# Moving modulation columns, key copies, spilled tiles and gate transposes in a two-block transformer kernel

## The chip, the cores and the metric

One core of a Trainium2 chip runs the whole kernel. The metric is the device time of one execution in microseconds, as a median over timed runs.

## The reference

Two transformer blocks are computed on a sequence of 512 rows of width 1024, in float32.

```python
c_act = silu(c)
for layer in range(2):
    mod = c_act @ ada_w[layer] + ada_b[layer]
    sh_m, sc_m, g_m, sh_f, sc_f, g_f = split(mod, 6)
    h = modulate(rms_norm(x, pre_mix_g), sh_m, sc_m)
    y = gmlp_mixer(h) if layer == 0 else fox_mixer(h, k, v, dcum)
    x = x + g_m * rms_norm(y, post_mix_g)
    h = modulate(rms_norm(x, pre_ffn_g), sh_f, sc_f)
    y = (silu(h @ w_gate) * (h @ w_up)) @ w_down
    x = x + g_f * rms_norm(y, post_ffn_g)
    if layer == 0:
        k, v, dcum = shared_kv(x, c_act @ kv_ada_w + kv_ada_b)
```

The hidden width of the FFN is 2816. `shared_kv` normalises and modulates x, multiplies it with the key, value and forget weights and normalises the keys per head. The second block follows: products for an mLSTM with four heads and for a sparse attention with eight heads whose keys an indexer picks, an output product, a gate, and a last norm.

## The kernel before

**Products.** Each float32 matrix is held as a high part (float32r, made by ScalarE) and a low part (the rest, made by VectorE's or GpSimd's subtraction). A product of two such matrices takes three matmuls (`mm3`, L414 to L416). `wsplit` (L277, L280) loads a weight chunk of 128x1024 from DRAM into one of four `raw` buffers and splits it into `whi` and `wlo`, each with four buffers; with `share=n`, GpSimd makes the low half of every n-th chunk. `gemm_a` keeps weights stationary and works output block by output block; one chunk is 24 matmuls of 128x512. `gemm_b` keeps the activations stationary: per group of 512 output columns it holds four accumulators, one for each 128 rows, and goes through chunks of 256 rows of the weight, 24 matmuls each. Its argument `then` runs a function after the first chunk of a group; `tail` chunks at the end are worked off row block by row block.

**Modulation columns.** `mod` is made column by column on VectorE: each of 112 columns is a load of 128x1024 (`ada_load`, L296, on SyncE's queue) and one multiply with sum over the free axis (`ada`, L300) into `modc`. Sixteen are made at the start. The other 96 go in the order of the list `ADA` and are spread over the products by `fill(n)`, which loads n columns into `raw` buffers per call and works off the columns loaded one earlier. In the first FFN's `gemm_a` each chunk from the eleventh on calls `fill(2)`; what is left is drained in a loop before the down product. The output product of the mixer, a `gemm_b`, calls `fill(1.5)`. `need` drains until eight named columns are there.

**FFN.** `ffn` multiplies with gate and up blocks in turn (`gemm_a`, 44 chunks). `evac` applies silu, multiplies (L603) and splits the result (L546, L548). Then `gemm_b` with the down weights follows, two groups of eleven chunks, with `post` as evacuation: norm, residual, norm of the next stage, and from every second row block transposes into `hk` (`to_T`). For the first FFN `to_T` also writes the normalised rows, transposed, to DRAM (`xT`, the spill).

**Shared keys and values.** `gemm_b` with the key weights (`headnorm` evacuates: L886 square, L888 sum, L889 copy, then a scaling of four tiles), then `forget` (L1111), then the eight spilled tiles: each is loaded from `xT` into a T tile (L1126), modulated on ScalarE (L1127), copied and subtracted on VectorE (L1128, L1129). Then `gemm_b` with the value weights. `kdone` transposes four pairs of heads, splits them into T tiles (L1082, L1083) and writes them with `spread` from GpSimd's queue (L941): each half (64 partitions) of the high and low tile is written twice, so that DRAM holds four ready tiles of 128x512 for each pair of heads. There are nine T tiles. `loader` (L953) fetches these tiles on SyncE for this pair and the next. The second block's attention does the same with six tiles per pair (`ev_a`, L1292, L1293, L941).

**Attention.** For each head: scores (L990, L991), softmax, transposes (L1017), values (L1032), with chunks of other products between them.

**Gates.** After the index product, a chain of small operations with two scans (L1264 to L1273) makes the gates `la` and `lt` in T tiles. `columns()` transposes the index weights (L1253) and then the gates (L1259), and is called after the first of the `w_aqk` chunks; the index scores (L1309 to L1317) follow the second.

**Order.** Each engine takes its instructions in a fixed order, settled when the program is built; a scheduler settles it from the program's order and its own costs, except in the parts that are written under a manual schedule. SyncE and GpSimd take their DMA issues in order too.

Of the kernel before, what the change touches and what calls it, by code (L numbers as in the profile page):

```python
# [40 lines left out]
GU = (2, 3)  # L41
GG = (1, 1)
DT = (4, 4)
DS = (0, 0)
# [3 lines left out]
IG = 1  # L48
# [141 lines left out]
def body(tc, nc, a):  # L190
    V, S_, G, PE = nc.vector, nc.scalar, nc.gpsimd, nc.tensor

    with ExitStack() as es:
# [99 lines left out]
        def ada_load(col, raw=None):  # L293
# [124 lines left out]
        def gemm_a(h, w, n, evac, m=P, group=0, nfill=0, share=0, gshare=1):  # L418
# [38 lines left out]
        def gemm_b(h, w, groups, kt, evac, head=False, tail=0, nfill=0, share=0, raws=(), hshare=1, then={}):  # L457
# [6 lines left out]
            for gi in groups:  # L464
# [125 lines left out]
        def ffn(l, h, xsrc, xdst, gb, nxt):  # L590
            with tc.tile_pool(name=f"f{l}", bufs=44) as pf:
# [346 lines left out]
        def spread(d, at, hi, lo):  # L938

            for q, (src, half) in zip(at, ((hi, TOP), (lo, TOP), (hi, BOT), (lo, BOT))):  # L940
                nc.gpsimd.dma_start(d[q].rearrange("(a p) n -> p a n", a=2),  # L941
                                    src[half].unsqueeze(1).broadcast_to((64, 2, 512)))

        def loader(alloc, src, n, last):
# [697 lines left out]
```

## Time and profile before

| | |
|---|---|
| Median of three timed runs | 1885.8 us |
| Lowest and highest | 1879.63 and 1886.22 us |
| Profiled execution | 1873.39 us, span 1871.5 us |
| Mean granted TensorE clock | 0.994 |
| TensorE busy | 1822.3 us (97%) |
| VectorE, ScalarE, GpSimd busy | 1126.0, 789.9, 357.9 us |
| DMA | 305.76 MB, 163 GB/s |

In the rows further down PE is TensorE's matmul, PEld its weight load, DVE is VectorE, ACT ScalarE, POOL GpSimd and SP SyncE; a small q behind the name is the engine's own queue of instructions. "out<-in" names the tiles that an instruction writes and reads, `<-` behind a wait names what ended it, and x counts instructions. Times are microseconds unless a row says ns.

### The profile page before, as it was taken

What the parts mean: (1) busy time and instruction counts of PE and PEld (TensorE: products, weight loads), DVE (VectorE), ACT (ScalarE), POOL (GpSimd) and SP (SyncE); (2) the same over time, 40 slices, a digit from 0 to 9 for tenths busy, and PEclk for the clock granted to TensorE, in tenths of its full rate; (3) what the DMA queues carried; (4) which work ended last, traced back from release to release, by engine and by line L of the source; (5) the groups of instructions that cost most, each with busy time, mean ns of one, the idle gap of its engine ahead of it and who ended that gap; (6) DMA issues with size and microseconds to landing.
All of it is one profiled execution on the core that took longest, in us unless ns stands there. A gap on an engine that the chain in (4) does not pass through costs nothing. (4 is left out here: it accounts for less than half of the span.)

```text
span 1871.5 us, 23902 instructions
## 1 busy us (share of the span) xinstructions
PE 1822.3 (97%) x8688; PEld 1504.1 (80%) x8688; DVE 1126.0 (60%) x2166; ACT 789.9 (42%) x1395; POOL 357.9 (19%) x294
## 2 busy tenths in 40 slices
PE   8999999999999999999999999999999999999997
PEld 5788888888777877787778888888887878888886
DVE  7869745577774256549876423332278978746534
ACT  5333324422222244558765322322256256455334
POOL 2000000222220023343331211100012562031022
PEclk9999999999999999999999999999999999999999
DMA  9674563587775437745533332332436553333532
GB/s 341 234 251 144 159 230 113 171 268 242 253 260 189 147 120 232 259 168 163 165 102 113 112 102 90 101 112 91 147 130 193 176 164 123 106 96 107 173 110 78
DMA packets 101969, 305.76 MB, mean 163 GB/s; under 512 B 12278, under 2 KB 13086, under 8 KB 101851
## 3 DMA queue, kind: packets, MB, share of 16 engines
q1 hardware_dynamic: 93402, 276.96, 44.7%
q0 software_dynamic: 8448, 27.27, 4.1%
q8 instruction: 69, 1.13, 0.2%
q14 instruction: 50, 0.40, 0.1%
HBM read 269.50 MB, written 37.30 MB: 164 GB/s over the span
## 5 line engine op out<-in xcount | busy, mean ns | idle before, releaser
L277 ACT ACTIVATE whi<-raw 128x1024 fp32r<-128x1024 f32 x281 | 296.7, 1058 | 644.2 <-PE acc L416 303.4
L280 DVE TENSOR_TENSOR wlo<-raw,whi 128x1024 fp32r<-128x1024 f32 x191 | 238.3, 1251 | 303.8 <-ACT whi L277 285.0
L414 PE MATMUL acc<-h,whi 128*128 128x512 f32 x896 | 350.5, 391 | 3.2 <-DVE t L603 2.6
L416 PE MATMUL acc<-h,wlo 128*128 128x512 f32 x896 | 349.5, 390 | 4.1 <-DVE wlo L280 4.0
L280 POOL TENSOR_TENSOR wlo<-raw,whi 128x1024 fp32r<-128x1024 f32 x90 | 221.7, 2465 | 673.0 <-ACT whi L277 593.7
L415 PE MATMUL acc<-h,whi 128*128 128x512 f32 x896 | 348.9, 389 | 0.0
L414 PE MATMUL acc<-whi,h 128*128 128x512 f32 x608 | 242.2, 399 | 8.8 <-DVE h L406 5.2
L415 PE MATMUL acc<-wlo,h 128*128 128x512 f32 x608 | 240.3, 396 | 1.4 <-POOL wlo L280 1.1
L416 PE MATMUL acc<-whi,h 128*128 128x512 f32 x608 | 240.1, 396 | 0.0
L416 PEld LDWEIGHTS acc<-h,wlo 128*128 128x128 f32 x896 | 168.2, 188 | 41.7 <-DVE wlo L280 6.6
L414 PEld LDWEIGHTS acc<-h,whi 128*128 128x128 f32 x896 | 168.3, 188 | 40.0 <-issue 5.3
L415 PEld LDWEIGHTS acc<-h,whi 128*128 128x128 f32 x896 | 168.3, 188 | 34.5
L300 DVE SCALAR_TENSOR_TENSOR raw<-raw,cact 128x1024 f32<-128x1024 f32 x96 | 146.4, 1536 | 76.7 <-DMA raw<-in_ada 73.9
L414 PE MATMUL acc<-whi,s 128*128 128x512 f32 (+1 forms) x488 | 190.6, 391 | 0.6 <-DVE t L1328 0.6
L415 PE MATMUL acc<-wlo,s 128*128 128x512 f32 (+1 forms) x488 | 190.9, 391 | 0.3 <-DVE wlo L280 0.3
L416 PE MATMUL acc<-whi,s 128*128 128x512 f32 (+1 forms) x488 | 190.2, 390 | 0.0
L414 PEld LDWEIGHTS acc<-whi,h 128*128 128x128 f32 x608 | 115.5, 190 | 33.6 <-DVE h L406 6.4
L416 PEld LDWEIGHTS acc<-whi,h 128*128 128x128 f32 x608 | 115.6, 190 | 26.0 <-DVE h L407 2.0
L415 PEld LDWEIGHTS acc<-wlo,h 128*128 128x128 f32 x608 | 115.7, 190 | 25.5 <-POOL wlo L280 1.9
L572 POOL DMA_DIRECT2D scr<-s x24 | 13.3, 556 | 541.5 <-DVE s L571 540.4
L414 PEld LDWEIGHTS acc<-whi,s 128*128 128x128 f32 x488 | 91.7, 188 | 20.4 <-DVE t L1328 1.0
L415 PEld LDWEIGHTS acc<-wlo,s 128*128 128x128 f32 x488 | 91.7, 188 | 19.3 <-DVE wlo L280 0.6
(371 smaller groups left out, 2779.4 us busy)
## 6 DMA issues: line engine op xcount, KB each, us to landing
raw<-in_ada SPq DMA_DIRECT2D x96, 512.0 KB, 4.1
raw<-in_w_gu SPq DMA_DIRECT2D x88, 512.0 KB, 4.0
raw<-in_w_dn SPq DMA_DIRECT2D x44, 512.0 KB, 3.4
scr<-t POOLq DMA_DIRECT2D x56, 256.0 KB, 5.6
raw<-in_w_o SPq DMA_DIRECT2D x20, 512.0 KB, 3.3
row<-scr SPq DMA_DIRECT2D x36, 256.0 KB, 2.7
d<-in_ada SPq DMA_DIRECT2D x16, 512.0 KB, 6.9
raw<-in_w_v SPq DMA_DIRECT2D x16, 512.0 KB, 4.7
```

The lines of the kernel that those rows point to most:

```text
L277: S_.activation(hi[:, 0:n], raw[:, 0:n], AF.Copy)
L280: e.tensor_sub(lo[:, 0:n], raw[:, 0:n], hi[:, 0:n].bitcast(F32))
L300: V.scalar_tensor_tensor(raw, raw, 1.0, cact[0], ALU.mult, ALU.mult, accum_out=modc[:, col:col + 1])
L414: PE.matmul(out, lh, rh, start=start, stop=False)
L415: PE.matmul(out, lh, rl, start=False, stop=False)
L416: PE.matmul(out, ll, rh, start=False, stop=stop)
L572: nc.gpsimd.dma_start(xdst[rows, h * 512:(h + 1) * 512], xr[h])
```

## The change

- **First FFN, gate and up.** VectorE makes all low halves (`GU[0]` from 2 to 0), and `fill` gets 1.625 columns per chunk instead of 2.
- **First FFN, down.** The loop that drained the rest of the columns moves from before the product into the evacuation's first call of `mod` (second group, first row block). The product calls `fill(1.5)`; its columns are loaded as two half tiles of 128x512 out of the H tiles, three columns ahead, and take two instructions and a sum.
- **Keys.** The high and low tile of a pair are written to DRAM whole, once (two writes instead of four). The loader puts the four (or six) tiles together out of half-tile loads.
- **Spilled tiles.** Three loads are issued before the value product; the modulation of two tiles goes behind the second and the third chunk of each of its two groups, and loads the next ones.
- **Gates.** The gates' transposes leave `columns()` and are called after the fourth `w_aqk` chunk instead of the first.
- Unused arguments (`gshare`, `DS`) go.

```diff
-GU = (2, 3)
+GU = (0, 3)
@@ ada_load, ada, fill
+        def ada_load(col, raw=None, half=None):
+            if half:
+                raw = [half(), half()]
+                for q in range(2):
+                    nc.sync.dma_start(raw[q], a["ada"][col][:, q * 512:(q + 1) * 512])
+                return col, raw
...
         def ada(col, raw):
+            if isinstance(raw, list):
+                s = small()
+                for q in range(2):
+                    V.scalar_tensor_tensor(raw[q], raw[q], 1.0, cact[0][:, q * 512:(q + 1) * 512], ALU.mult, ALU.mult,
+                                           accum_out=s[:, q:q + 1])
+                V.tensor_add(modc[:, col:col + 1], s[:, 0:1], s[:, 1:2])
+                return
...
-        def fill(n=1):
+        def fill(n=1, half=None, depth=1):
...
-                    held.append(ada_load(ADA[ada_next[0]]))
-                if len(held) > 1 or ada_next[0] >= len(ADA) and held:
+                    held.append(ada_load(ADA[ada_next[0]], half=half))
+                if len(held) > depth or ada_next[0] >= len(ADA) and held:
@@ gemm_b
-                    if 0 < c < nch - 1:
-                        fill(nfill)
+                    if 0 < c < nch - (2 if half else 1):
+                        fill(nfill, half, 3 if half else 1)
                     for t in range(NT):
                         part(t, c, wh, wl)
                     if c == 0 and gi in then:
                         then[gi]()
+                    if each:
+                        each(c)
@@ ffn
-                gemm_a(h, a[f"w_gu{l}"], 2 * KF, evac, group=4, nfill=2, share=GU[l], gshare=GG[l])
-                while len(done) < len(ADA):
-                    fill()
+                gemm_a(h, a[f"w_gu{l}"], 2 * KF, evac, group=4, nfill=1.625, share=GU[l])
                 gb = gb()
-                gemm_b((hh, hl), a[f"w_dn{l}"], range(2), KF, post(gb, xsrc, xdst, F, nxt()), tail=DT[l], share=DS[l])
+                gemm_b((hh, hl), a[f"w_dn{l}"], range(2), KF, post(gb, xsrc, xdst, F, nxt()), tail=DT[l], nfill=1.5, half=None if l else lambda: H(F32))
@@ nxt0
-            hk.extend(hpair())
-            return halves(hk, lambda: (gain(104, "kvg"), need(96)), xT)
+            def mod():
+                while len(done) < len(ADA):
+                    fill()
+                hk.extend(hpair())
+                return gain(104, "kvg"), need(96)
+            return halves(hk, mod, xT)
@@ loader, kdone
-                        for q in range(n):
-                            nc.sync.dma_start(got[p_][q].bitcast(F32), src[p_, q])
+                        for q, half, s in src(p_):
+                            nc.sync.dma_start(got[p_][q][half].bitcast(F32), s)
...
+        def keys(d, at):
+            return [(at[2 * hv + q], ot, d[q, me]) for hv, me in enumerate((TOP, BOT)) for q in range(2) for ot in (TOP, BOT)]
...
-                    spread(kscr[pr], range(4), hi.bitcast(F32), lo.bitcast(F32))
+                    for q, part in enumerate((hi, lo)):
+                        nc.gpsimd.dma_start(kscr[pr, q], part.bitcast(F32))
@@ spilled tiles
-            for j in range(KD):
-                f = T()
-                nc.sync.dma_start(f, xT[j])
-                S_.activation(f, f, AF.Identity, scale=gm[:, j:j + 1], bias=sm[:, j:j + 1])
-                V.tensor_copy(hx[0][j], f)
-                V.tensor_sub(hx[1][j], f, hx[0][j].bitcast(F32))
+            def unspill(c):
+                if c in (0, 3):
+                    return
+                for _ in range(2):
+                    j = len(hdone)
+                    hdone.append(j)
+                    f = spilled[j]
+                    S_.activation(f, f, AF.Identity, scale=gm[:, j:j + 1], bias=sm[:, j:j + 1])
+                    V.tensor_copy(hx[0][j], f)
+                    V.tensor_sub(hx[1][j], f, hx[0][j].bitcast(F32))
+                    if len(spilled) < KD:
+                        spill_load()
+            hdone = []
+            for _ in range(3):
+                spill_load()
             gemm_b(hk, a["w_vv"], range(2), KD, lambda g, t, pt: vsplit(g, t, pt, va, vdone),
-                   then={0: lambda: kdone(1)})
+                   then={0: lambda: kdone(1)}, each=unspill)
@@ ev_a
+                for q, part in enumerate((hi, lo)):
+                    nc.gpsimd.dma_start(d[2 * (i % 2) + q], part)
                 if i == 0:
                     columns()
+                if i == 3:
+                    gates_T()
```

## Rows read from the trace of the kernel before

**Rows 1.** Page, part 1: each engine's busy time, share of the span, instructions.

```profile
PE 1822.3 (97%) x8688; PEld 1504.1 (80%) x8688; DVE 1126.0 (60%) x2166; ACT 789.9 (42%) x1395; POOL 357.9 (19%) x294
```

**Rows 2.** Windows: stretch, its length, busy time (instructions), granted clock, DMA share, GB/s.

```profile
core 0: us, PE busy (x) PEld busy (x) DVE busy (x) ACT busy (x) POOL busy (x), PEclk, DMA share, GB/s
233.00:266.00 33.00, 33.00 (x148) 27.31 (x147) 15.08 (x20) 6.37 (x6) 0.00 (x0) 1.00 0.75 256
374.00:467.60 93.60, 93.60 (x414) 77.54 (x413) 71.30 (x92) 24.91 (x32) 21.25 (x8) 1.00 0.80 255
490.00:570.00 80.00, 73.15 (x308) 56.69 (x308) 60.76 (x80) 19.55 (x26) 14.41 (x6) 1.00 0.79 259
571.00:680.00 109.00, 108.73 (x479) 89.27 (x479) 33.94 (x35) 29.63 (x40) 0.34 (x1) 1.00 0.41 137
```

**Rows 3.** Waits of TensorE, 470 to 570 us: total, times, longest.

```profile
PE acc L416 <- DVE wlo L280: 4.0, 5, 1.0
PE acc L414 <- DVE t L603: 2.6, 5, 1.3
```

**Rows 4.** Timeline of GpSimd and VectorE, 484 to 512 us: start, duration, instruction.

```profile
484.67 2.40 POOL L280 TENSOR_TENSOR wlo<-raw,whi 128x1024 fp32r<-128x1024 f32 x1 [10.18 <-ACT whi L277]
497.25 2.41 POOL L280 TENSOR_TENSOR wlo<-raw,whi 128x1024 fp32r<-128x1024 f32 x1 [10.18 <-ACT whi L277]
510.04 2.41 POOL L280 TENSOR_TENSOR wlo<-raw,whi 128x1024 fp32r<-128x1024 f32 x1 [10.38 <-ACT whi L277]
...
484.75 3.40 DVE L300 SCALAR_TENSOR_TENSOR raw<-raw,cact 128x1024 f32<-128x1024 f32 x1 [0.20 <-DMA raw<-in_ada]
491.50 1.22 DVE L300 SCALAR_TENSOR_TENSOR raw<-raw,cact 128x1024 f32<-128x1024 f32 x1 [0.20 <-DMA raw<-in_ada]
495.77 1.22 DVE L280 TENSOR_TENSOR wlo<-raw,whi 128x1024 fp32r<-128x1024 f32 x1
```

**Rows 5.** Waits of SyncE's queue, 330 to 580 us.

```profile
SPq L296 <- DVE raw L300: 134.6, 57, 3.3
```

**Rows 6.** Timelines of SyncE, ScalarE and TensorE, 728 to 753 us.

```profile
739.60 9.90 SPq L1126 DMA_DIRECT2D t<-scr  x4
...
744.01 0.82 ACT L1127 ACTIVATE t<-t,modc,gcol 128x512 f32<-128x512 f32 x1 [8.61 <-DMA t<-scr]
751.73 0.58 ACT L889 ACTIVATE k<-acc 128x512 f32<-128x512 f32 x1
...
752.36 0.80 PE L414 MATMUL acc<-whi,h 128*128 128x512 f32 x1 [3.54 <-ACT k L889]
```

**Rows 7.** Windows around the lower clock, columns as in rows 2.

```profile
752.00:753.50 1.50, 1.14 (x3) 0.95 (x4) 1.50 (x3) 1.50 (x4) 0.00 (x0) 0.50 1.01 350
753.50:758.00 4.50, 4.50 (x12) 3.53 (x11) 4.12 (x9) 4.50 (x9) 0.00 (x0) 0.50 0.73 255
```

**Rows 8.** Waits of TensorE, 1410 to 1428 us.

```profile
PE tp L1259 <- DVE t L1269: 2.2, 1, 2.2
```

**Rows 9.** Groups of instructions by line: busy us, mean ns, idle before.

```profile
L571 DVE SCALAR_TENSOR_TENSOR s<-t,sm,s 128x512 f32<-128x512 f32 x24 | 17.2, 748 | 0.5 <-DVE sm L358 0.3
```

**Rows 10.** DMA issues: count, KB each, median us to landing.

```profile
scr<-t POOLq DMA_DIRECT2D x56, 256.0 KB, 5.6
scr<-s POOLq DMA_DIRECT2D x24, 256.0 KB, 2.5
k<-scr SPq DMA_DIRECT2D x32, 256.0 KB, 4.5
scr<-t POOLq DMA_DIRECT2D x16, 128.0 KB, 3.5
```

**Rows 11.** SyncE, 820 to 985 us: its waits, and the last key loads.

```profile
SPq L953 <- PE tp L991: 20.8, 7, 6.9
...
909.00 3.68 SPq L953 DMA_DIRECT2D k<-scr  x4
920.86 0.32 SPq L953 DMA_DIRECT2D k<-scr  x1
```

More of the change, by code (lines that the diff above doesn't have):

```diff
@@ L47 @@
 OS = 3
-IG = 1
 MQ = 0
@@ L416, in mm3, with gemm_a @@
             PE.matmul(out, ll, rh, start=False, stop=stop)
-        def gemm_a(h, w, n, evac, m=P, group=0, nfill=0, share=0, gshare=1):
+        def gemm_a(h, w, n, evac, m=P, group=0, nfill=0, share=0):
             hi, lo = h
@@ L455, in gemm_a, with gemm_b @@
                 i += len(run)
-        def gemm_b(h, w, groups, kt, evac, head=False, tail=0, nfill=0, share=0, raws=(), hshare=1, then={}):
+        def gemm_b(h, w, groups, kt, evac, head=False, tail=0, nfill=0, share=0, raws=(), hshare=1, then={}, each=None, half=None):
             hi, lo = h
@@ L936, in stack @@
             return s0, s1
[L938 to L942, printed above, removed]
         def loader(alloc, src, n, last):
@@ L1083, in kdone @@
                     V.scalar_tensor_tensor(lo, pt, kgain[:], hi.bitcast(F32), ALU.mult, ALU.subtract)
-                    spread(kscr[pr], range(4), hi.bitcast(F32), lo.bitcast(F32))
-            kload = loader(lambda dt: tile_of(px, "k", dt, bufs=NKB), kscr, 4, 8)
+                    for q, part in enumerate((hi, lo)):
+                        nc.gpsimd.dma_start(kscr[pr, q], part.bitcast(F32))
+            kload = loader(lambda dt: tile_of(px, "k", dt, bufs=NKB), lambda pr: keys(kscr[pr], range(4)), 4, 8)
             def va(q, t):
@@ L1123, in body, with spill_load @@
             gm, sm = gain(56, "pmg1"), need(48)
[L1124 to L1129 removed]
+            spilled = []
+            def spill_load():
+                spilled.append(T())
+                nc.sync.dma_start(spilled[-1], xT[len(spilled) - 1])
+            def unspill(c):
[13 more added lines that the diff above has]
+                spill_load()
             gemm_b(hk, a["w_vv"], range(2), KD, lambda g, t, pt: vsplit(g, t, pt, va, vdone),
[L1131 removed]
+                   then={0: lambda: kdone(1)}, each=unspill)
             def qa(g, t):
@@ L1241, in ev_ix @@
                     V.tensor_scalar_add(gt[0][64:128], pt[64:128], vc("bgate", 0)[64:128, :])
-            gemm_a(h, a["w_ix"], 5, ev_ix, group=4, gshare=IG)
+            gemm_a(h, a["w_ix"], 5, ev_ix, group=4)
             g = gt[0]
@@ L1254, in columns @@
                 V.tensor_copy(iw[:], pt[:, 0:48].rearrange("p (t h) -> p t h", t=NT)[:, :, 4:12])
-                pt = tp()
-                for q, src in enumerate((la, lt)):
-                    for t in range(NT):
-                        o_ = (q * NT + t) * 4
-                        PE.transpose(pt[:, o_:o_ + 4], src[0:4, t * P:(t + 1) * P], ident[0:4, 0:4])
-                V.tensor_copy(am[:], pt[:, 0:32].rearrange("p (q t h) -> p q t h", q=2, t=NT))
-                S_.activation(am[:, 1, :, :], am[:, 1, :, :], AF.Exp, scale=-1.0)
             lf, lt, la, lm, on = T(), T(), T(), T(), T()
@@ L1275, in body, with gates_T @@
             am = pc.tile([P, 2, NT, 4], F32, name="am")
+            def gates_T():
+                pt = tp()
+                for q, src in enumerate((la, lt)):
+                    for t in range(NT):
+                        o_ = (q * NT + t) * 4
+                        PE.transpose(pt[:, o_:o_ + 4], src[0:4, t * P:(t + 1) * P], ident[0:4, 0:4])
+                V.tensor_copy(am[:], pt[:, 0:32].rearrange("p (q t h) -> p q t h", q=2, t=NT))
+                S_.activation(am[:, 1, :, :], am[:, 1, :, :], AF.Exp, scale=-1.0)
             av = {}
@@ L1288, in ev_a @@
                 d = ascr[i // 2]
-                if i % 2 == 0:
-                    for q, half in enumerate((TOP, BOT)):
-                        ot = (BOT, TOP)[q]
-                        nc.gpsimd.dma_start(d[3 * q, half], hi[half])
-                        nc.gpsimd.dma_start(d[3 * q, ot], lo[half])
-                else:
-                    spread(d, (1, 2, 4, 5), hi, lo)
+                for q, part in enumerate((hi, lo)):
+                    nc.gpsimd.dma_start(d[2 * (i % 2) + q], part)
                 if i == 0:
                     columns()
+                if i == 3:
+                    gates_T()
             gemm_a(h, a["w_aqk"], 2, ev_a, share=2)
@@ L1378, in ev_z, with qsrc @@
                 nc.sync.dma_start(gscr[t, g], s)
-            qkload = loader(qk2, ascr, 6, 4)
+            def qsrc(pr):
+                d = ascr[pr]
+                return ([(0, TOP, d[0, TOP]), (0, BOT, d[1, TOP]), (3, BOT, d[0, BOT]), (3, TOP, d[1, BOT])]
+                        + keys(d[2:4], (1, 2, 4, 5)))
+            qkload = loader(qk2, qsrc, 6, 4)
             def aprep(pr):
```

7 lines of the change are left out of this document (2 added, 5 removed).

## The prediction

> **What bounds the kernel now.** I read the page's first part first: TensorE is busy 97% of the span [rows 1], so only time in which TensorE waits, or runs at the lower clock, can be won. Busy time flatters a pipelined engine, so I then counted matmuls by stretch. A free stretch (374 to 467.6) does 414 matmuls in 93.60 us, 0.226 us each [rows 2]. I looked for stretches under that rate next to a line of the change, and then asked the waits and the timelines why. Three are found.
>
> First, the gate and up product of the first FFN. Between 490 and 570 us there are 308 matmuls, worth 308 x 0.226 = 69.6 us, in 80.0: 10.4 us lost [rows 2]. TensorE waits there for VectorE alone, for a low half or for an evacuation [rows 3]. The timeline says why VectorE is late: per pair of chunks it works through four columns of the modulation, GpSimd makes one of the two low halves in 2.40 us, and the column beside that takes 3.40 us instead of 1.22 [rows 4]. GpSimd's halves come 12.6 and 12.8 us apart, so a pair takes 12.7 us where 48 matmuls need 48 x 0.226 = 10.85. SyncE waits, between 330 and 580, 134.6 us for column buffers that VectorE has not released [rows 5]: columns and weights share four. The stretch before (374 to 467.6) runs the same loop without a loss; buffers filled earlier carried it.
>
> Second, the start of the value product in the shared keys and values. SyncE holds the loads of the spilled activations, since their T tiles still wait for the key writes; ScalarE, which has the modulation of the spilled tiles ahead of the norm of the key product, waits 8.61 us for one of them; the evacuation at L889 comes late and TensorE waits 3.5 us for it [rows 6]. [...]
>
> Third, the gates' transposes: TensorE waits 2.2 us for the scan chain on VectorE [rows 8].
>
> **The change part by part.** The sum is made against the profiled execution, 1873.4 us (span 1871.5). The three timed runs have a median of 1885.8, 12.4 above it; I carry the difference over to the timed runs. A measurement of this kernel can tell about 0.5% from no change, 9.4 us.
>
> *Columns and low halves in gate/up.* By the code 34 chunks fetch 1.625 columns instead of 2, 55 instead of 68, and VectorE makes all low halves. Per pair VectorE loses one blocked column's excess (3.40 - 1.22 = 2.18) and 0.75 columns (0.75 x 1.22 = 0.92), and gains one low half (1.22): 1.88 less, where 1.85 are lost per pair. If not VectorE's work but the ring of four buffers sets the pace, a pair has 5.25 uses instead of 6: 12.7 x 5.25 / 6 = 11.1 us, 0.26 above 10.85, over 17 pairs 4.4 us, part of it covered by the buffers filled earlier. So the gain lies between 6.0 and 10.4 us. I take 9.5, near the upper end, since both causes are relieved together. What hides the added low halves is VectorE's idle time: 60.8 of 80 us are busy [rows 2].
>
> *Columns in the down product.* By the code 16 columns are loaded there in halves and 17 worked off, mostly 1.5 per chunk of 24 matmuls (5.4 us). A column costs two half products, about 0.75 each by the nearest 128x512 instruction of this form [rows 9]: 1.5 us and a small sum, some 27 us in all, on an engine that is busy 33.9 of 109 us there now [rows 2]. The nearest row for the traffic is the output product of the mixer (233 to 266), the same loop shape with the same 1.5 columns per chunk: 148 matmuls in 33.0 us at 256 GB/s, nothing lost [rows 2]. The other bound is the loss rate of 490 to 570, 10.4 in 80, over 14 chunks: 9.9 us. I take 0, by the row that has the same shape. The halves lie in the H tiles that the product before has just left, so SyncE may wait at the first of them for the last gate/up chunk; behind it stand the weights of the third chunk, needed 16 us later. The drain that stood between the products, four fills, goes into the first evacuation of the second group, and by the code nothing is left to drain then. The transposes of the gate row stay.
>
> *Spilled activations.* The eight loads and their 24 instructions leave the place ahead of the value product; two go behind the second and third chunk of each group, three loads being issued ahead. Gone are the 3.5 us wait and half of the 6 us at the lower clock [rows 7], 3.0: together 6.5. What is late next: two modulations of 0.8 us each per place on ScalarE, ahead of a weight's high half that is split a chunk early, so hidden. The five later loads stand on SyncE among weights that have their own buffers. I take 6.0, because the three loads ahead still queue for T tiles as now. The ends are 6.5 won, and each of the four places costing what the one costs now: 4 x 6.5 - 6.5 = 19.5 lost.
>
> *Keys in DRAM once.* Key writes fall from 32 to 16 in the first attention and from 32 to 16 in the second; a whole-tile write from 128 partitions lands in 2.5 us, the present 256 KB ones in 5.6 [rows 10]. So T tiles come free earlier, a cover for the part above. The loads grow from 56 of 256 KB to 112 of 128 KB. One issue holds SyncE 0.32 us, so 56 x 0.32 = 18 us more on that queue over both attentions, with weights and rows behind. Now the key loads of the first attention wait for TensorE, 20.8 us in all, to release the tiles of a pair that is done [rows 11], so they are early. I take 0. Ends: 1 us won through the writes, and 45 lost, worked out as a rival below.
>
> *Gates' transposes.* They go three chunks back, behind the index scores: the 2.2 us wait goes, eight small transposes stay. The two gate tiles stay held meanwhile, so ScalarE has two fewer of nine T tiles for the scores. I take 2.0, between 2.2 and 1.0 lost.
>
> Removed arguments and the constants of the second FFN change no instruction.
>
> Sum: 9.5 + 0 + 6.0 + 0 + 2.0 = 17.5 us. 1873.4 - 17.5 = 1855.9 for the profiled execution, and 1885.8 - 17.5 = 1868.3 for the median.
>
> **The rivals.**
>
> *Half-tile loads come late, slower.* Place: the scores of both attentions. A 128 KB write from 64 partitions lands in 3.5 us, a 256 KB one from 128 in 2.5 [rows 10]: half the partitions are no faster per tile. If a pair's loads, now 4.5 us, took twice that and nothing hid it, ten later pairs would lose 4.5 each: 45 us, 1868.3 + 45 = 1913. It decides once a pair's loads take longer than their lead. The loads of the last two pairs begin at 909.00 and 920.86, 11.9 us apart [rows 11], and each begins while the pair ahead of it is still to be worked on, so 9 us should hide. Chance 0.04.
>
> [...]
>
> *The stall moves house.* The columns starve the down product as they starve gate/up: 9.9 us lost there, 1868.3 + 9.9 = 1878.2. For it: 1.5 columns and a chunk's weights are 1.31 MB per 5.4 us, 243 GB/s, close to the 259 of the starved stretch. Against it: the row at 256 GB/s without loss, and a pool of sixteen half tiles apart from the weights' four. Chance 0.14.
>
> *The spilled loads stall four times.* They come late in each middle chunk and hold ScalarE: 1868.3 + 6.0 + 19.5 = 1893.8. For it: the T tiles are short there (nine, of which the second half of the keys wants eight). Against it: three are loaded ahead and the key writes are halved. Chance 0.06.
>
> *The order does less than it says.* The instruction order of each engine is fixed when the program is built; if gate/up stays at the ring's pace and the spilled part keeps half its cost, the gain is 6.0 + 3.0 + 1.0 = 10.0: 1875.8. Chance 0.13.
>
> **How the numbers follow.** The forecast, 1868.3, has 0.63. Its own range goes from all terms at their best (10.4 + 6.5 + 1 + 2.2 = 20.1, 1865.7) to 1874, and the runs of one kernel differ: the fastest timed one is 6.2 under the median, the profiled one 12.4. So the low end is 1856. The high end takes in the last case and the stall that moves house with some spread: 1885. Left out are the slow rivals and the tails, under 2 in 10. Faster by over 0.5% (under 1876.4): nearly all of the forecast and most of the last case, 0.71. Within 0.5%: the moved stall, half of the four stalls, a rest of the others, 0.24. Slower by over 0.5% (over 1895.2): 0.05.
>
> **What would show it.** In the profile of the changed kernel the gate/up stretch should run at 0.226 us per matmul to its end, the column instruction at 1.22 us throughout, and GpSimd should make no low half there. The down product should hold over 250 GB/s in its first group with no wait of TensorE for a low half. At the value product no wait for L889 should stand and the granted clock should stay at 1.00. The wait of the gates' transposes should be gone. I am wrong if TensorE waits for low halves in the down product, if ScalarE waits for spilled tiles in the middle chunks, or if a score matmul waits for a key load.

## The result, and the profile after

The changed kernel takes **1862.72 us** (median of 4 runs, 1861.47 to 1864.74); the kernel before, run beside it, 1882.72 (4 runs, 1878.15 to 1886.22). The ratio is 0.9897, 95% interval 0.9877 to 0.9917: faster by about 1%, 20.0 us between the medians. The profiled execution took 1861.47 us (span 1859.5); that of the kernel before 1873.39.

So two profiles show only 11.9 us of the 20.0. TensorE's last matmul ends at 1861.11 us before and at 1851.71 after, 9.4 earlier; the other 2.5 lie in the tail behind it, which belongs to the keys (see the part on the prediction). To see where the 9.4 come from I added up, along each trace, what successive matmul starts are apart beyond the median for their shape (0.23 us for 128x512, 0.11 to 0.12 for small transposes), leaving out what is under 0.03 us. "Lost" below means that sum for a stretch; another choice of the usual distance moves it by up to half a microsecond.

| Stretch | Lost before | Lost after |
|---|---|---|
| Gate/up product of the first FFN | 10.4 | 0 |
| Start of the value product | 7.2 | 5.5 |
| Gates and index scores | 4.7 | 6.2 |
| First 67 us of the sparse attention | 6.5 | 7.5 |

**Engines.** Page, part 1, of the changed kernel, beside [rows 1]:

```profile
PE 1819.8 (98%) x8688; PEld 1507.4 (81%) x8688; DVE 1116.0 (60%) x2234; ACT 790.9 (43%) x1395; POOL 287.8 (15%) x242
```

GpSimd is busy 70.1 us less; VectorE is not busier, although it makes 20 more low halves: its columns are no longer stretched.

**Gate/up.** Windows of the changed kernel over the stretches of [rows 2], with the same columns:

```profile
233.00:266.00 33.00, 33.00 (x147) 27.31 (x147) 15.01 (x20) 6.37 (x6) 0.00 (x0) 1.00 0.76 253
374.00:467.60 93.60, 93.60 (x414) 77.52 (x413) 60.68 (x91) 26.30 (x33) 0.00 (x0) 1.00 0.72 234
490.00:570.00 80.00, 80.00 (x354) 66.03 (x354) 53.84 (x89) 23.85 (x31) 0.00 (x0) 1.00 0.77 254
571.00:680.00 109.00, 109.00 (x489) 90.06 (x488) 48.40 (x108) 30.35 (x50) 2.28 (x5) 1.00 0.50 174
```

Between 490 and 570 us there are 354 matmuls, not 308: the free rate to the end. The waits of TensorE in [rows 3] have no successor between 470 and 570. The column's line, 470 to 680 us (shortest, median and longest duration in ns):

```profile
L309 DVE SCALAR_TENSOR_TENSOR raw<-raw,cact x23: 1215/1224/1227, 469.3 to 548.2; 128x1024 f32<-128x1024 f32 x23
```

No column is stretched; before, the longest took 3402 ns, as in [rows 4]. SyncE's waits, 330 to 580 us, the answer to [rows 5]:

```profile
SPq L266 <- DVE raw L309: 67.8, 27, 4.5
SPq L298 <- DVE raw L309: 50.1, 21, 4.4
```

Together 117.9 us for weights and columns. Before, the columns waited 134.6 us [rows 5] and the weights (L269) another 15.4 for the same line, 150.0 together. So 117.9 us of such waits stand in a stretch that loses nothing: a queue that runs ahead waits for buffers all the time, and the size of this row was no sign of a loss.

**Value product.** First SyncE's and ScalarE's timeline, 717 to 763 us, the answer to [rows 6]:

```profile
717.53 7.46 SPq L1142 DMA_DIRECT2D t<-scr  x3
...
751.70 3.36 SPq L1142 DMA_DIRECT2D t<-scr  x5
...
758.01 3.10 ACT L1152 ACTIVATE t<-t,modc,gcol 128x512 f32<-128x512 f32 x4 [5.97 <-DMA t<-scr]
761.01 1.04 ACT L274 ACTIVATE whi<-raw 128x1024 fp32r<-128x1024 f32 x1
761.96 0.80 ACT L1152 ACTIVATE t<-t,modc,gcol 128x512 f32<-128x512 f32 x1
762.66 0.36 ACT L918 ACTIVATE v<-acc 128x256 fp32r<-128x256 f32 x1
```

The first three loads go out from 717.53 on and cost TensorE nothing. The five later loads of spilled tiles do not go out two by two behind middle chunks; they are issued together from 751.70 on. ScalarE waits 5.97 us for the first of them, then has four modulations in a row and a fifth behind a weight's high half, and only then evacuates the first group. TensorE's wait, 730 to 775 us, and the window at the lower clock, with the columns of [rows 7]:

```profile
PE acc L423 <- DVE v L920: 3.6, 2, 3.3
```

```profile
765.95:769.36 3.41, 3.19 (x8) 2.08 (x7) 3.38 (x10) 1.74 (x4) 0.37 (x2) 0.50 0.44 139
```

The wait of 3.54 us and some 6 us at granted clock 0.50 [rows 7] have become a wait of 3.3 us and 3.4 us at 0.50, some 13 us later.

**Gates.** Waits of TensorE, 1395 to 1425 us, and of ScalarE, 1400 to 1420 us, the answer to [rows 8]:

```profile
PE tp L1339 <- ACT t L1342: 2.5, 2, 1.8
PE tp L1283 <- ACT t L1276: 1.2, 1, 1.2
...
ACT t L1342 <- DVE t L562: 1.9, 1, 1.9
ACT t L1342 <- DVE t L1293: 1.6, 1, 1.6
```

The 2.2 us at the transposes are gone. The index scores, now ahead of them, wait 2.5 us for ScalarE's relu (L1342), which itself waits for a T tile that an earlier chunk (L562) or the gates' chain (L1293) still holds.

**Keys.** DMA issues of the changed kernel, the answer to [rows 10] (count, KB each, median us to landing):

```profile
scr<-t POOLq DMA_DIRECT2D x40, 256.0 KB, 3.9
k<-scr SPq DMA_DIRECT2D x64, 128.0 KB, 3.8
qk<-scr SPq DMA_DIRECT2D x48, 128.0 KB, 3.4
```

All 256 KB writes of such tiles land in 3.9 us instead of 5.6 (both counts hold the eight writes of the spill), the half-tile key loads in 3.8 where whole tiles took 4.5.

### The profile page after: what moved, and what is told of

The parts are those of the page before. It is cut to its first block, busy times and chain, and to the rows that moved or that the text cites. A ratio compares the mean times of both kernels' runs of the same rounds, so it can differ in the third digit from the quotient of the medians.

```text
span 1859.5 us, 24012 instructions
## 1 busy us (share of the span) xinstructions
PE 1819.8 (98%) x8688; PEld 1507.4 (81%) x8688; DVE 1116.0 (60%) x2234; ACT 790.9 (43%) x1395; POOL 287.8 (15%) x242
## 4 chain that ended last, share of the span: by engine, by line
PE 85%; DVE 9%; ACT 3%; issue 1%; DMA 1%; POOL 0%; SPq 0%; ACTq 0%; DVEq 0%; POOLq 0%
PE acc L423 24%; PE acc L425 24%; PE acc L424 24%; PE tp L1045 2%; DVE d L309 1%; PE tp L1030 1%; PE acc L460 1%; PE acc L455 1%; PE acc L454 1%; PE tp L391 1%; PE tp L1003 1%; PE tp L846 1%; DVE wlo L277 1%; PE tp L1004 1%; DVE s L1373 0%
## 5 line engine op out<-in xcount | busy, mean ns | idle before, releaser
L277 DVE TENSOR_TENSOR wlo<-raw,whi 128x1024 fp32r<-128x1024 f32 x211 | 262.5, 1246 | 289.7 <-ACT whi L274 262.4
L277 POOL TENSOR_TENSOR wlo<-raw,whi 128x1024 fp32r<-128x1024 f32 x70 | 171.1, 2445 | 498.1 <-ACT whi L274 433.3
L309 DVE SCALAR_TENSOR_TENSOR raw<-raw,cact 128x1024 f32<-128x1024 f32 x80 | 97.7, 1223 | 96.4 <-DMA raw<-in_ada 96.2
L423 PEld LDWEIGHTS acc<-whi,s 128*128 128x128 f32 x488 | 91.7, 188 | 19.9 <-DVE t L1358 0.9
L425 PEld LDWEIGHTS acc<-whi,s 128*128 128x128 f32 x488 | 91.7, 188 | 18.8
```

The costliest lines, as they stand in the source:

```text
L277: e.tensor_sub(lo[:, 0:n], raw[:, 0:n], hi[:, 0:n].bitcast(F32))
L423: PE.matmul(out, lh, rh, start=start, stop=False)
L425: PE.matmul(out, ll, rh, start=False, stop=stop)
```

## The experiments

Twelve runs were made: parts of the change on the kernel before, the changed kernel with a part undone, and extra work on GpSimd. Ratios are to the kernel before, run beside each. All compute the same; the two with extra work say so. The runs come from several sessions, in which the median of the kernel before lay between 1878.67 and 1882.72 us, so times of different sessions can be compared to some 4 us only: experiments 1 to 4 are one session, 5 to 8 another, 9, 10 and 12 a third, and 11 and the changed kernel one each. Line numbers shift by a few between kernels.

**1. The kernel before, again.** No edit.

> The kernel before, unchanged, for a second profile. The medians of the two kernels lie 20.0 us apart, their profiled executions 11.9. If the gate and up product is what varies from run to run, because its column loads wait on the memory, a profile of an execution near 1882 us shows about 18 us lost there instead of 10.4, and the value product's 6.5 us unchanged. The rival: the rest varies (lower clock after other waits, the start), and the gate and up product loses 10.4 again.

Measured: 1880.26 us (1874.76 to 1886.45, 10 runs), ratio 0.9994 (0.998 to 1.0008). The profiled execution took 1882.80, 9.4 more than the first profile. Its gate/up window:

```profile
490.00:570.00 80.00, 73.08 (x309) 56.70 (x308) 58.75 (x81) 19.38 (x25) 14.56 (x7) 1.00 0.76 255
```

309 matmuls, as in [rows 2]: the loss there is the same, as the rival said. What this execution loses more lies in pieces of 1 to 3 us elsewhere (1.1 at 273 us, 1.8 at the gate row at 574, 2.3 at the gates). Executions of this kernel differ by over 10 us, and not through gate/up alone.

**2. Low halves alone.**

```diff
-GU = (2, 3)
+GU = (0, 3)
```

> The kernel before with one constant changed: VectorE makes all low halves of the first gate and up product; columns stay at 2 per chunk. If GpSimd's hold on VectorE (3.40 instead of 1.22 us for one column in four) is the cause, most of the stall goes: 6 to 10 us faster, column instructions at 1.22 us throughout. If the ring of four buffers or the bytes set the pace, it stays: six buffer uses per pair at 2.1 us each, 0 to 2 us faster, or slower since VectorE has 1.2 us more per pair.

Measured: 1865.91 us (1864.93 to 1867.48, 4 runs), ratio 0.9913 (0.9898 to 0.9927): 14.5 us, about three quarters of the whole gain, from one constant. Gate/up, still with two columns per chunk:

```profile
490.00:570.00 80.00, 80.00 (x355) 66.13 (x354) 58.43 (x89) 23.74 (x31) 0.00 (x0) 1.00 0.84 273
```

Nothing lost at 273 GB/s: the ring of four buffers carries six uses per pair of chunks and more bytes than before. By itself it was not a limit.

**3. Columns alone.** The kernel before with 1.625 columns per chunk, the rest in half tiles in the down product; GpSimd keeps its low halves.

```diff
-                gemm_a(h, a[f"w_gu{l}"], 2 * KF, evac, group=4, nfill=2, share=GU[l], gshare=GG[l])
-                while len(done) < len(ADA):
-                    fill()
+                gemm_a(h, a[f"w_gu{l}"], 2 * KF, evac, group=4, nfill=1.625, share=GU[l], gshare=GG[l])
                 gb = gb()
-                gemm_b((hh, hl), a[f"w_dn{l}"], range(2), KF, post(gb, xsrc, xdst, F, nxt()), tail=DT[l], share=DS[l])
+                gemm_b((hh, hl), a[f"w_dn{l}"], range(2), KF, post(gb, xsrc, xdst, F, nxt()), tail=DT[l], share=DS[l], nfill=1.5, half=None if l else lambda: H(F32))
... (ada_load, ada, fill, gemm_b and nxt0 as in the change)
```

> The kernel before with the columns alone moved (1.625 per chunk in gate and up, the rest as half tiles in the down product); GpSimd still makes every second low half. Ring theory: 5.25 uses per pair at 2.1 us make 11.1 us per pair against 10.85: 7 to 10 us faster. Blocked-column theory: only 0.92 of the 1.85 us per pair goes: 4 to 6 us faster. Both: the down product shows no wait of TensorE for a low half.

Measured: 1884.72 us (1877.34 to 1890.15, 10 runs), ratio 1.001 (0.999 to 1.003). VectorE and GpSimd around 505 us, then TensorE's waits from 423 to 570 us:

```profile
505.33 3.36 DVE L312 SCALAR_TENSOR_TENSOR raw<-raw,cact 128x1024 f32<-128x1024 f32 x1 [1.68 <-issue]
...
505.22 2.40 POOL L280 TENSOR_TENSOR wlo<-raw,whi 128x1024 fp32r<-128x1024 f32 x1 [10.27 <-ACT whi L277]
```

```profile
PE acc L428 <- DVE wlo L280: 15.9, 10, 3.4
```

Neither expected gain (7 to 10 us, 4 to 6 us) came: fewer columns do not help while one in each pair is held. This execution (1890.15) loses even more in gate/up than the one before.

**4. The change without its FFN parts.** Columns and low halves as before; keys, spilled tiles and gates as changed.

```diff
-GU = (0, 3)
+GU = (2, 3)
...
-                gemm_a(h, a[f"w_gu{l}"], 2 * KF, evac, group=4, nfill=1.625, share=GU[l])
+                gemm_a(h, a[f"w_gu{l}"], 2 * KF, evac, group=4, nfill=2, share=GU[l])
+                while len(done) < len(ADA):
+                    fill()
                 gb = gb()
-                gemm_b((hh, hl), a[f"w_dn{l}"], range(2), KF, post(gb, xsrc, xdst, F, nxt()), tail=DT[l], nfill=1.5, half=None if l else lambda: H(F32))
+                gemm_b((hh, hl), a[f"w_dn{l}"], range(2), KF, post(gb, xsrc, xdst, F, nxt()), tail=DT[l])
```

> The changed kernel with both FFN parts undone; keys, spilled tiles and gates as changed. The profiles of the two kernels give these three together about 1.5 us (the value product 1.7 better, the gates 0.9 worse, the rest level), so 0 to 3 us faster than before. If instead they carry part of the 8 us by which the medians differ more than the profiles, 6 to 10 us faster.

Measured: 1874.39 us (1870.58 to 1887.04, 10 runs), ratio 0.9975 (0.9955 to 0.9996): 6.0 us from the other three parts together, the second of the two expectations; the interval leaves 0.8 to 8.5 us. With experiment 2 that is 14.5 + 6.0 = 20.5, about what the whole change brings.

**5. The change with columns as before.** Two columns per chunk and the drain; low halves on VectorE.

```diff
-                gemm_a(h, a[f"w_gu{l}"], 2 * KF, evac, group=4, nfill=1.625, share=GU[l])
+                gemm_a(h, a[f"w_gu{l}"], 2 * KF, evac, group=4, nfill=2, share=GU[l])
+                while len(done) < len(ADA):
+                    fill()
                 gb = gb()
-                gemm_b((hh, hl), a[f"w_dn{l}"], range(2), KF, post(gb, xsrc, xdst, F, nxt()), tail=DT[l], nfill=1.5, half=None if l else lambda: H(F32))
+                gemm_b((hh, hl), a[f"w_dn{l}"], range(2), KF, post(gb, xsrc, xdst, F, nxt()), tail=DT[l])
```

> The changed kernel with the columns put back: 2 per chunk in gate and up, the rest drained between the two products, no half tiles in the down product; VectorE still makes all low halves. If the columns matter beside the low halves, gate and up loses 2 to 10 us again and this is that much slower than the changed kernel (1865 to 1873). If GpSimd's hold was all, it is level: 1861 to 1865.

Measured: 1863.56 us (1862.68 to 1865.3, 4 runs), ratio 0.9892 (0.9864 to 0.992): level with the change. The medians lie 0.8 us apart, which these runs cannot tell from nothing.

**6. The change with the spilled tiles as before.**

```diff
-            spilled = []
... (spill_load, unspill, three loads)
+            for j in range(KD):
+                f = T()
+                nc.sync.dma_start(f, xT[j])
+                S_.activation(f, f, AF.Identity, scale=gm[:, j:j + 1], bias=sm[:, j:j + 1])
+                V.tensor_copy(hx[0][j], f)
+                V.tensor_sub(hx[1][j], f, hx[0][j].bitcast(F32))
             gemm_b(hk, a["w_vv"], range(2), KD, lambda g, t, pt: vsplit(g, t, pt, va, vdone),
-                   then={0: lambda: kdone(1)}, each=unspill)
+                   then={0: lambda: kdone(1)})
```

> The changed kernel with the spilled tiles put back ahead of the value product. By the profiles that place cost 7.2 us before and 5.5 after, so the step is worth 1.7: this comes 1 to 3 us slower, 1864 to 1866, with the wait at the copy of the key product back. The rival: with half the key writes the T tiles come free sooner, the old order stalls less than before, and this is level or faster (1858 to 1862).

Measured: 1861.97 us (1861.07 to 1863.85, 4 runs), ratio 0.9884 (0.9856 to 0.9912): level, as the rival said. TensorE's waits in this kernel, 735 to 775 us:

```profile
PE acc L423 <- DVE v L920: 0.8, 1, 0.8
PE tp L975 <- DVE k L908: 0.8, 3, 0.3
```

With the keys written once the *old* order loses 2.9 us here, the new one 5.5. In these two profiles the 2.6 us are given back in the attention that follows. Its window, 817 to 966 us, first in this kernel, then in the changed one:

```profile
817.00:966.00 149.00, 141.00 (x763) 114.49 (x762) 129.29 (x438) 115.07 (x264) 52.03 (x28) 1.00 0.46 146
```

```profile
817.00:966.00 149.00, 143.47 (x776) 116.53 (x776) 127.79 (x441) 116.24 (x266) 52.98 (x28) 1.00 0.47 150
```

The value product and this attention together lose 22.5 us here and 22.8 in the changed kernel, so their sum is level too.

**7. The change with the gates as before.**

```diff
                 if i == 0:
                     columns()
-                if i == 3:
                     gates_T()
```

> The changed kernel with the gates' transposes back behind the first chunk. If holding two T tiles longer costs what the profiles show (a wait of 2.5 us of the index scores and a spell at the lower clock, against 2.2 us before), this is level or up to 2 us faster: 1860 to 1863. If the step gains what I forecast, it is 2 us slower.

Measured: 1863.4 us (1858.48 to 1866.74, 4 runs), ratio 0.9882 (0.9846 to 0.9917): level, in runs that lie 8 us apart and so cannot show 2 us. The old wait is back, the one at the index scores is gone (waits of TensorE, 1395 to 1425 us):

```profile
PE tp L1306 <- DVE t L1292: 2.2, 1, 2.2
```

**8. The change with the keys as before.** Written twice by 64 partitions at a time, loaded whole.

```diff
-for q, part in enumerate((hi, lo)):
-    nc.gpsimd.dma_start(kscr[pr, q], part.bitcast(F32))
+spread(kscr[pr], range(4), hi.bitcast(F32), lo.bitcast(F32))
...
-for q, half, s in src(p_):
-    nc.sync.dma_start(got[p_][q][half].bitcast(F32), s)
+for q in range(n):
+    nc.sync.dma_start(got[p_][q].bitcast(F32), src[p_, q])
... (the same for ev_a's tiles in the second attention)
```

> The changed kernel with the keys written out ready-made, four (six) tiles a pair, and loaded whole. If the half-tile loads cost nothing and the writes only free T tiles sooner, this is slower by what the value product then loses: 0 to 4 us, 1862 to 1867. The rival (loads over 64 partitions come late): this is faster than the changed kernel, with shorter waits in both attentions.

Measured: 1877.89 us (1876.57 to 1885.81, 10 runs), ratio 0.998 (0.9961 to 0.9999). This one undo costs 15.2 us, far more than the 0 to 4 expected. The timelines of GpSimd and ScalarE, 745 to 775 us, and the window of the stall:

```profile
766.35 0.61 POOL L955 DMA_DIRECT2D scr<-t  x1 [0.93 <-DMA scr<-t]
...
771.28 0.81 ACT L1157 ACTIVATE t<-t,modc,gcol 128x512 f32<-128x512 f32 x1 [13.59 <-DMA scr<-t]
```

```profile
766.00:784.00 18.00, 4.31 (x11) 3.14 (x10) 9.65 (x26) 7.87 (x14) 0.61 (x1) 0.63 0.73 258
```

GpSimd still issues key writes until 766.35, the last ones with pauses in which it waits for an earlier one to land. ScalarE's modulation waits 13.59 us, which the profile puts down to such writes; the evacuation of the value product stands behind it. TensorE does 11 matmuls in 18 us, and the start of the value product loses 16.0 us.

**9. Keys and spilled tiles both as before.** The edits of 6 and 8 together.

> The changed kernel with two steps undone together: the keys are written twice and loaded whole as before, and the spilled tiles are modulated ahead of the value product as before. Theory (the two steps hang on each other): with the spread keys alone the changed kernel lost 15 us, because the modulation's tiles stood behind key writes; with the old order of the spilled tiles that wait cannot fall into the value product, so the time is about 1866 to 1868 us, the one stall of about 7 us ahead of the value product back. Rival (writing the keys twice costs 15 us wherever the spilled tiles stand): about 1877 us, as with the keys alone undone.

Measured: 1866.12 us (1864.58 to 1867.14, 4 runs), ratio 0.9933 (0.9916 to 0.9949). Waits of TensorE, 735 to 760 us:

```profile
PE acc L423 <- ACT k L903: 4.6, 1, 4.6
```

The old stall, the one of [rows 6], at the old place. So writing the keys twice does not cost 15 us by itself; the two parts hang on each other:

| | Spilled tiles ahead | Spilled tiles behind middle chunks |
|---|---|---|
| Keys written twice | 1866.12 (lost 8.3) | 1877.89 (lost 16.0) |
| Keys written once | 1861.97 (lost 2.9) | 1862.72 (lost 5.5) |

In brackets, what TensorE loses at the start of the value product. Keys once gain 4.2 us with the old order. The new order of the spilled tiles costs 11.8 with the keys written twice and nothing measurable with them written once. The four times come from three sessions: by the ratios to the kernel before, 0.9933 against 0.9884 and 0.998, the 4.2 would be some 9 and the 11.8 some 9, so that the sizes are rough and the pattern holds.

The link can be read from SyncE's waits for the spilled loads. In the kernel before, 675 to 830 us:

```profile
SPq L1126 <- DVE hm L1129: 13.7, 3, 7.0
SPq L1126 <- DMA scr<-t: 1.4, 1, 1.4
```

The loads wait 13.7 us for VectorE's last instruction on an earlier spilled tile, and only 1.4 us for key writes, so that they go out one behind another over 22 us. The same two waits are 14.9 and 1.5 us in this kernel, and 12.5 and 5.4 in experiment 8. With the keys written once and the old order (experiment 6) they are 0.8 and 5.8, and all eight loads go out within 11 us. Why the built order makes spilled tiles follow one another in the same T tiles when the keys are written twice is not shown.

**10. Extra GpSimd work, small.** Extra work that nothing reads: three 128x256 subtractions beside each second chunk of gate/up.

```diff
-GU = (2, 3)
+GU = (0, 3)
...
+                    if n == 2 * KF and share == 0 and i % 2 == 0:
+                        wf = ws[0][0].bitcast(F32)
+                        for q in range(3):
+                            G.tensor_sub(gj[:], wf[:, q * 256:(q + 1) * 256], wf[:, 768:1024])
```

> The kernel before, with no low half of the gate/up product on GpSimd, but with three 128x256 subtractions on GpSimd beside each second chunk that read two inputs from SBUF and write a tile that nothing reads (extra work, the outputs are the same). Theory (GpSimd's work by itself holds VectorE's modulation columns): columns beside it lengthen again, from 1.22 us to about 2.5 to 3.5, stalls of TensorE come back at 490 to 570 us, and the time is 1874 to 1882 us. Rival (what cost the time was TensorE's dependence on the slow low half, GpSimd's 2.40 us against 1.22 on VectorE, and the raw buffers that it kept): columns may lengthen or not, no stall of TensorE comes back, and the time is about 1866 us as with the low halves moved alone.

Measured: 1866.34 us (1863.62 to 1867.7, 4 runs), ratio 0.9931 (0.9917 to 0.9946). GpSimd and VectorE:

```profile
485.22 4.09 POOL L432 TENSOR_TENSOR gj<-whi 128x256 bf16<-128x256 f32 x3 [7.34 <-ACT whi L278]
...
485.52 1.52 DVE L301 SCALAR_TENSOR_TENSOR raw<-raw,cact 128x1024 f32<-128x1024 f32 x1 [0.32 <-DMA raw<-in_ada]
487.36 1.36 DVE L301 SCALAR_TENSOR_TENSOR raw<-raw,cact 128x1024 f32<-128x1024 f32 x1 [0.32 <-DMA raw<-in_ada]
488.65 1.75 DVE L281 TENSOR_TENSOR wlo<-raw,whi 128x1024 fp32r<-128x1024 f32 x1
```

The time is the rival's, but the test was too weak for it: columns took at most 1.81 us and low halves 1.75, not 3.40, and TensorE had no wait there. These GpSimd instructions, three in 4.09 us, held VectorE in short pieces only.

**11. Extra GpSimd work, full.** The very subtraction that GpSimd did before, in two halves, into tiles that nothing reads.

```diff
-GU = (2, 3)
+GU = (0, 3)
...
-                    ws.append(wsplit(w[i], KD * m, share))
+                    raw = load_w(w[i], KD * m)
+                    ws.append(wsplit(w[i], KD * m, share, raw=raw))
+                    if n == 2 * KF and share == 0 and i % 2 == 0:
+                        for q in (slice(0, 512), slice(512, 1024)):
+                            G.tensor_sub(T(F32R), raw[:, q], ws[0][0][:, q].bitcast(F32))
```

> The kernel before, with all low halves of the gate/up product on VectorE, and beside each second chunk GpSimd does the very subtraction that it did before, raw minus high half, 128x1024 in two halves, into tiles that nothing reads (extra work, the outputs are the same). So GpSimd reads the same two inputs and keeps the raw buffer as long as before; what is left out is that TensorE waits for its result. Theory (GpSimd holds VectorE, and with it the column and the chunk behind it): columns beside it take 2.8 to 3.4 us as before, TensorE stalls about 8 to 10 us between 470 and 570 us, and the time is 1874 to 1882 us. Rival (the hold costs nothing as long as TensorE's own low halves do not come from GpSimd, since VectorE has some 40 us to spare there): the columns lengthen all the same, TensorE's stalls stay under 2 us, and the time is 1864 to 1868 us, as with the low halves moved alone.

Measured: 1893.13 us (1892.25 to 1894.07, 4 runs), ratio 1.0069 (1.0051 to 1.0087), 27 us above experiment 2 and above both expected ranges. Timelines of GpSimd, VectorE, SyncE and ScalarE around 495 us, the window, and ScalarE's waits from 380 to 570 us:

```profile
492.07 4.55 POOL L431 TENSOR_TENSOR t<-raw,whi 128x512 fp32r<-128x512 f32 x2 [9.05 <-ACT whi L277]
...
493.17 2.30 DVE L300 SCALAR_TENSOR_TENSOR raw<-raw,cact 128x1024 f32<-128x1024 f32 x1
495.41 2.30 DVE L300 SCALAR_TENSOR_TENSOR raw<-raw,cact 128x1024 f32<-128x1024 f32 x1
...
495.51 2.56 SPq L296 DMA_DIRECT2D raw<-in_ada  x2
499.48 0.33 SPq L269 DMA_DIRECT2D raw<-in_w_gu  x1
...
490.94 1.06 ACT L277 ACTIVATE whi<-raw 128x1024 fp32r<-128x1024 f32 x1 [4.93 <-DMA raw<-in_w_gu]
```

```profile
490.00:570.00 80.00, 73.34 (x298) 53.56 (x296) 62.83 (x81) 20.77 (x26) 27.53 (x13) 1.00 0.74 246
```

```profile
ACT whi L277 <- DMA raw<-in_w_gu: 126.7, 29, 5.6
```

No matmul reads GpSimd's result, and yet 298 x 0.226 = 67.3 of 80 us are left: 12.7 lost, more than the 10.4 of before; at the start of the down product, 582 to 595 us, another 9.4 are lost. Another 4.0 at 273 to 281 lie ahead of the first extra subtraction (345.9 us), so that work did not cause them directly. TensorE need not depend on GpSimd's result: the work beside it is enough. The chain can be read off: a column held by GpSimd gives its buffer back late; SyncE's next loads, in order, are columns (495.51) with a weight behind them (499.48); ScalarE waits for weights, 126.7 us here against 29.4 in experiment 2 in the same stretch. The size is not that of before: two halves took 4.55 us here, one low half 2.40 [rows 4], two columns were stretched per pair, and GpSimd keeps T tiles and the chunk's raw buffer meanwhile. No wait of SyncE between 380 and 570 us ends on GpSimd and 118.3 us end on columns, which speaks for the hold on VectorE; but no run takes it apart from the tiles that GpSimd keeps.

**12. Other tiles for spilled tiles and gates.** The changed kernel, spilled tiles in tiles of the later values and queries, gates' chain in another pool.

```diff
-spilled.append(T())
+spilled.append(tile_of(px, "v" if len(spilled) < 4 else "q", bufs=8))
-for _ in range(3):
+for _ in range(4):
-lf, lt, la, lm, on = T(), T(), T(), T(), T()
+lf, lt, la, lm, on = (Z() for _ in range(5))
```

> The changed kernel, with the spilled tiles loaded into tiles of the later values and queries (free at that time, so four loads go out ahead and none waits for a key's tile), and with the gates' five chain tiles from another pool. Theory (the stall of 5.5 us in the value product comes from loads that wait for tiles that the key path holds, and 1 us of the gates from tiles the index relus want): the value product's stall falls to under 2 us, the index scores' wait to under 1, and the time is 1856 to 1859 us, 3 to 6 below the changed kernel. Rival (the DMA queues are full in this stretch, or the time goes back in the attention that follows): the stall moves and the time is 1861 to 1865, level with the changed kernel.

Measured: 1862.02 us (1861.37 to 1864.44, 4 runs), ratio 0.9913 (0.9898 to 0.9927): level with the change, so the rival holds. SyncE's timeline, 745 to 755 us, and the waits of the engines, 730 to 775 us:

```profile
745.98 3.43 SPq L962 DMA_DIRECT2D k<-scr  x4
749.51 1.03 SPq L1142 DMA_DIRECT2D q<-scr  x2
...
752.12 2.30 SPq L1142 DMA_DIRECT2D q<-scr  x2
```

```profile
ACT q L1152 <- DMA q<-scr: 6.2, 2, 5.0
...
PE acc L423 <- DVE v L920: 3.2, 1, 3.2
```

The last four loads go out from 749.5 and 752.1 on all the same, behind key loads in SyncE's queue, and the stall stays (6.1 us lost). The T tiles are not what makes these loads late once the keys are written once. At the gates TensorE's wait for L1342 fell from 2.5 to 1.4, too little to be seen in the time. Whether an order written out by hand would keep the modulations apart was not tried.

No kernel here is measurably faster than the changed one.

## Why the prediction was right, and where not

The forecast of 1868.3 lay 5.6 above the result, inside its range, with the sign right. The largest step was right; that the sum came so near was luck, as two misses of opposite sign met in it. Step by step:

- **Gate/up, 9.5 of 6.0 to 10.4: right, at the upper end.** All 10.4 us lost before are gone. But the ground for "near the upper end, since both causes are relieved together" was wrong: there was one cause, GpSimd's work beside VectorE's. Relieving the ring alone gains nothing (experiment 3), moving the low halves alone gains all (2), and putting GpSimd's work back without its result brings a loss of that kind back, and a larger one (11). The trace shows the hold in time: in the kernel before, the eight columns that start between 470 and 570 us beside one of GpSimd's low halves take 2.85 to 3.40 us, and each ends 1.08 us after it, as the one in [rows 4] does; the 25 others that start in that stretch take 1.21 to 1.23.
- **Columns in the down product, 0: right.** No wait of TensorE there, so the stall did not move house (the rival at 1878.2). The expected 250 GB/s and more in its first group did not come: 178 GB/s in 580 to 630 us; the cover was ampler than reckoned.
- **Spilled tiles, 6.0 won: wrong.** Measured nothing (6), and 11.8 lost without the change to the keys (8 and 9). The reading behind it was off already: the loads were said to be held "since their T tiles still wait for the key writes", but only 1.4 us of SyncE's waits end on key writes and 13.7 on an earlier spilled tile (9). The step that failed is "two modulations of 0.8 us each per place on ScalarE, ahead of a weight's high half that is split a chunk early, so hidden", with five loads "on SyncE among weights". The built order put five loads and five modulations together in front of the first evacuation: ScalarE waits 5.97 us for a spilled tile there, a sign that the prediction had named for being wrong, and the granted clock, which was to stay at 1.00, falls to 0.50. The rival of four stalls had the mechanism, a modulation that waits for its load and holds ScalarE; it came once, not four times.
- **Keys once, 0: wrong in size.** Measured 4.2 us won with the old order of the spilled tiles (6 and 9), 15.2 with the new one (8). The prediction named a cause, "T tiles come free earlier, a cover for the part above", but gave it no price. It left out another: from the end of the last matmul to the end of the span pass 10.4 to 10.5 us in the eight profiles of kernels that write the keys twice, and 7.8 in the six of kernels that write them once. In the profiles of 9 and 6 the last matmul ends at the same time, 1852.9 us, so this tail is all that they differ by. What fills it is not shown; in the kernel before SyncE is done with its instructions at 1868.0 us and GpSimd's next one stands at 1870.8, in the changed kernel at 1858.6 and 1858.8. The rival in which half-tile loads come late (1913) did not happen: no score matmul waits for a load in either attention, and the half-tile loads land in 3.8 and 3.4 us, not later than whole ones (4.5).
- **Gates, 2.0 won: not seen.** Undone, the time is level (7). The step that failed is "the 2.2 us wait goes": it goes at the transposes and comes back as 2.5 us at the index scores, where ScalarE lacks T tiles; that was the reason given for the lower end, 1.0 lost. In the first two profiles the stretch loses 1.5 more, but over all of them it loses 4.7 to 7.1 us with the old place of the transposes (seven profiles) and 4.9 to 7.3 with the new one (seven).
- **The sum and what was carried over.** For the profiled execution 17.5 us were forecast and 11.9 came. The median came out near only because another step failed the other way: the 12.4 us between profile and median were carried over, while the changed kernel's profile lies 1.25 under its median. The first profile of the kernel before was simply a fast execution: no timed run here of that kernel was as fast. Whether the spread goes with GpSimd's low halves is not shown: experiments 1, 3 and 4, which have them, spread over 12 to 16 us in 10 runs each, and 2, 5, 6 and 9 over 3 in 4 runs each, but 7 and 8 without them over 8 and 9, and 11, with more GpSimd work, over 2. Where the spread sits in the kernel before stays open; in its second profile it was not in gate/up (1).

By the single parts: 14.5 (2) + 4.2 (6, 9) + 0.8 (5) + 0.7 (7) - 0.8 (6) = 19.4, against 20.0 measured. Only the first term stands clear of the differences between sessions; the rest says that the other parts bring a few microseconds together.

## What to carry to other kernels

When a slow engine's help stretches a neighbour's instructions, price the help by what the neighbour loses and by what stands behind that in an in-order queue, not by the busy time it takes over. Parts of a change that share tiles are not priced one by one: undo each alone and the two together before saying what one is worth. And a profile that is faster than every timed run is not the kernel's usual execution; the difference need not carry over.

## What the runs showed of the hardware

GpSimd's own instructions suffer as well: the 40 subtractions of 128x512 in experiment 11 took 1.28 us at the shortest and 2.27 at the median, while VectorE's columns beside them took 2.30 instead of 1.22. Beside one 128x1024 GpSimd instruction of 2.40 us [rows 4] the column took all the delay, 3.40 us; beside the shorter ones both engines paid.

Writes that were half as many also landed sooner. The 256 KB writes from T tiles between 700 and 790 us, the first attention's key writes and four of the spill, took 7.7 us to land at the median in the kernel before (36) and 6.9 in experiment 8 (36), both writing keys twice, against 4.5 in the changed kernel (20). How much of that is the number and how much the form (whole tiles instead of 64 partitions twice) is not told apart.
